# AdaLN modulation columns computed by a multiply-and-sum on VectorE, with most lower weight parts split off on GpSimd

## The chip, the cores and the metric

The kernel runs on one core of a Trainium2 chip, in float32. The metric is the device time of one execution in microseconds (us). The engines are TensorE (PE, matrix products; PEld is its weight load), VectorE (DVE), ScalarE (ACT) and GpSimd (POOL). Weights are fetched by DMA from one queue that SyncE (SP) issues in order.

## The reference

Two transformer blocks over one sequence of 256 tokens and 1024 features. What the change touches is the modulation at the head of each block: one row `c` of 1024 numbers, times a 1024x6144 matrix, gives six vectors.

```
mod = silu(c) @ ada_w + ada_b                       # 6 x 1024
sh1, sc1, g1, sh2, sc2, g2 = split(mod, 6)
h = rmsnorm(x, norm_mix) * (1 + sc1) + sh1
x = x + g1 * (diff_attention(h) @ w_out)            # block 1: qkv = h @ w_in, 8 heads
h = rmsnorm(x, norm_ffn) * (1 + sc2) + sh2
x = x + g2 * hier_moe(h)                            # 16 experts, top 2 of the best group
# then a final rmsnorm, and block 2 in the same shape with c_2, ada_w_2:
# w_in_2, sparse attention and RWKV-7 side by side, w_out_2, MoE of 32 experts
```

## The kernel before

**Layout.** Activations stand feature by feature: 128 features on the partitions, eight column blocks, 256 tokens. The parts sh1, sc1, g1, sh2 and sc2 are therefore wanted as columns (feature on the partition, in the tile `mod`), and only the last gain g2 as a row (`gt`). Memory is cut into 21 units of 128x2048 floats (NU); `Stream` (L98) loads weight tiles of up to 1 MB into slots made of units, each DMA issued on SP (L128) in program order. A load waits until the readers of what its slot held before are done, and everything behind it on SP waits with it.

**Products in three.** A float32 product is done as three faster products on high and lower parts. For block 1's `w_in` and `wo` tiles, `Splits.split` (L619) copies a piece to its high part on ACT (L628) and subtracts for the lower part (L629), on the engine that the plan's letter names: "v" is DVE, "g" is POOL. The plan is "vg": half of each tile on either engine.

**Modulation.** A job is 512 outputs. At the start of block 1, `matvec_rows` (L404) multiplies on PE (L410), ACT copies the row out (L413), PE transposes it (L425) and DVE sums it to columns (L427, L428). From there on `matvecs` (L432) does the jobs beside the heads, by letter: "t" on PE (L467, with an ACT copy), "v" as eight scalar-times-row steps of 128x512 on DVE (L460, then L462). Either leaves rows, which `to_columns` (L481) turns to columns by 128x1 matmuls (L487) and a small DVE sum (L488). In block 2 (parts 2, 4, 3 and the gains) all is "v", with tiles quartered to 128x1024 (0.5 MB) and two slots.

**Stages.** (1) Norm of x and, in two halves over the contraction, the projection to the first half of q, k and v (`first_half`, L746; `ready`, L1370 makes the modulated activation: L587, L591 to L596). (2) From 81 us, `weave` (L137) interleaves the eight heads, `sum_up` (L1404, the modulation jobs, in its last part jobs2(0, 1) for block 2) and `dense` (the rest of the projection, L798, then the first part of the output projection, L908). It orders the work by costs that each generator yields; a negative yield (lead, wait) spends time without work. (3) Output projection and routing from 208 us, then 16 experts from 245 us. (4) Block 2's mixer from 490 to 882 us. There `conditions` weaves the remaining jobs beside selection, heads and RWKV-7. (5) From 882 us on, 32 experts, whose 176 tiles of 1 MB are fetched behind a flag that SP reads (a branch on whether a slot overflowed).

Of the kernel before, what the change touches and what calls it, by code (L numbers as in the profile page):

```python
# [16 lines left out]
P = 128  # L17
# [379 lines left out]

def silu_cond(c, name):
    t = c.const.tile([P, KD], F32, name="cond_" + name)
    c.nc.scalar.activation(t, c.col[name], AF.Silu)  # L400
    return t


def matvec_rows(c, cond, ws):  # L404

    nc = c.nc
    ps = bank(c)
    for k in range(KD):
        g = k % 4
        nc.tensor.matmul(ps[32 * g:32 * g + 32, :], cond[:, k:k + 1].to_broadcast([P, 32]),  # L410
                         ws[k // 4][:, k % 4, :], start=k < 4, stop=k >= 4)
    row = c.small.tile([P, 512], F32, name="mvsum", bufs=1)
    nc.scalar.copy(row, ps)  # L413
    return row


def matvec(c, cond, names, bcol, out):

    nc = c.nc
    for i, nm in enumerate(names):  # L420
        row = matvec_rows(c, cond, [c.st.get(nm + "a"), c.st.get(nm + "b")])
        yield 2.0
        pt = bank(c)
        for b in range(4):
            nc.tensor.transpose(pt[:, b * P:(b + 1) * P], row[:, b * P:(b + 1) * P], c.ident)  # L425
        o = out[:, 4 * i:4 * i + 4]
        nc.vector.tensor_reduce(o, pt.rearrange("p (b g m) -> p b g m", b=4, g=4)[:, :, :, 0], AX.X, ALU.add)  # L427
        nc.vector.tensor_tensor(o, o, bcol[:, 4 * i:4 * i + 4], ALU.add)  # L428
        yield 0.4


def matvecs(c, cond, st, jobs, engs, lead, wait, rows, parts):  # L432

    nc = c.nc
    V = nc.vector
    names = [n + h for n, _ in jobs for h in parts]
    kn = KD // len(parts)
    ahead, left = [], []  # L440

    def sink():
        f, mine, eng = left.pop(0)
        yield from f(mine, c.c32[:, 0:1] if eng == "t" else c.ones[:, 0:1])

    for (_, f), eng in zip(jobs, engs):
        mine = []
        for h in range(len(parts)):
            while names and len(ahead) < len(st.slots):
                ahead.append(st.get(names.pop(0)))  # L450
            yield -lead
            w = ahead.pop(0)
# [20 lines left out]
            if h == 0 and left:  # L473
                yield from sink()
        left.append((f, mine, eng))
        if len(rows) == 1 or f is jobs[-1][1]:
            yield -wait
            yield from sink()


def to_columns(c, bcol, out):  # L481

    def sink(rows, one):
        pt = bank(c)
        for b in range(4):
            for i, row in enumerate(rows):
                c.nc.tensor.matmul(pt[:, b:b + 1], row[:, b * P:(b + 1) * P], one[:row.shape[0]], start=i == 0, stop=i == len(rows) - 1)  # L487
        c.nc.vector.tensor_tensor(out, pt[:, 0:4], bcol, ALU.add)  # L488
        yield 1.2
    return sink  # L490

# [278 lines left out]
def attention1(c, x, o, qkv, ap, sps, pop):  # L770
# [75 lines left out]
    def norm(po, al):  # L846
# [494 lines left out]
def block1(c, xT):  # L1341
    nc, tc, st, I = c.nc, c.tc, c.st, c.I
    mod = c.const.tile([P, 48], F32, name="mod1")
    bcol = c.col["ada_b"]
    cond = silu_cond(c, "c")

    def mv(*parts, hs=(0, 1)):
        for i in parts:
            for h in hs:
                o = slice(8 * i + 4 * h, 8 * i + 4 * h + 4)  # L1350
                yield from matvec(c, cond, [f"ada{2 * i + h}"], bcol[:, o], mod[:, o])
    m = lambda i: mod[:, 8 * i:8 * i + 8]
# [704 lines left out]
def block2(c, acc, out):  # L2057
# [40 lines left out]
    with tc.tile_pool(name="hp2", bufs=1) as hp, tc.tile_pool(name="rp", bufs=1) as rp:  # L2098
# [50 lines left out]
        def conditions():  # L2149
# [88 lines left out]
def tiles():  # L2238

    it = {}
    a = slice(None)

    def w(name, key, *at, k=KD):
        assert name not in it
        it[name] = key, at, k

# [4 lines left out]
    for b, x in (("a", ""), ("b", "_2")):  # L2253
        for i in range(12):
            cs = slice(512 * i, 512 * (i + 1))
            if b == "a" or i < 4:
                for h in range(2):
                    w(f"ad{b}{i}{'ab'[h]}", f"ada_w{x}", (slice(512 * h, 512 * (h + 1)), cs), k=4)
            else:
                for h in range(4):  # L2260
                    w(f"ad{b}{i}{h}", f"ada_w{x}", (slice(256 * h, 256 * (h + 1)), cs), k=2)
    for p in range(3):
# [23 lines left out]
    for pfx, n, x in (("x", 16, ""), ("y", 32, "_2")):  # L2286
# [7 lines left out]
        for q in range(2):  # L2294
# [29 lines left out]
def lay_out(inputs):  # L2324
# [52 lines left out]
def build(tc, I, out):  # L2377
# [4 lines left out]
    with tc.tile_pool(name="const", bufs=1) as c.const, \  # L2382
# [31 lines left out]
```

## Time and profile before

| | us |
|---|---|
| median of 3 runs (lowest to highest) | 1343.98 (1343.59 to 1347.93) |
| the profiled execution: its own time | 1341.36 |
| its span | 1339.8 |

| engine | busy us | share of the span |
|---|---|---|
| PE | 1146.8 | 86% |
| DVE | 592.5 | 44% |
| ACT | 347.0 | 26% |
| POOL | 101.7 | 8% |
| 16 DMA engines | mean 302 GB/s, 404.09 MB | |

The granted TensorE clock was 0.941 of full speed over the span. The busy shares are means over stages with different limits, so they are read stage by stage: a window's row gives the busy time of each engine in that window. A timeline row gives start, duration, engine, line, operation, output<-inputs and shape; xN means N instructions in a run, and what stands in brackets is the idle time before the first and what ended it.

### The profile page before, as it was taken

The numbers are of one execution on the slowest core, as the hardware profiler recorded it, in microseconds if no ns is written. First come the engines' busy times: TensorE is split into PE (matmuls) and PEld (weight loads), VectorE is DVE, ScalarE is ACT, GpSimd is POOL, SyncE is SP. The second block draws the span as 40 slices with busy tenths as digits, with TensorE's granted clock in tenths as the row PEclk, the third lists the DMA queues.
The fourth block names the chain that finished last, engine by engine and source line by source line (L and its number), as shares of the span: only waits on it lengthen the run. The fifth ranks groups of instructions, "written<-read, shape, count | busy, mean of one in ns | idle before, by whom it ended". The sixth has DMA issues, their size and how long they took to land. (4 is left out here: it accounts for less than half of the span.)

```text
span 1339.8 us, 20574 instructions
## 1 busy us (share of the span) xinstructions
PE 1146.8 (86%) x8434; PEld 705.4 (53%) x8434; DVE 592.5 (44%) x1464; ACT 347.0 (26%) x675; POOL 101.7 (8%) x111
## 2 busy tenths in 40 slices
PE   5899977899998986988999999889876797677775
PEld 2777767444434335876788888844332242233221
DVE  4477653333225137698555747343222222222212
ACT  3335331211111124552232224232111111111111
POOL 2421110000001003002410010000000000000000
PEclk7999978899999996999999999989889988999898
DMA  8777756699996953350135628769999999999996
GB/s 302 288 276 267 277 223 274 282 418 419 420 384 246 418 218 123 127 187 34 64 140 208 205 94 331 281 256 417 420 419 420 419 420 420 419 420 418 421 419 267
DMA packets 60516, 404.09 MB, mean 302 GB/s; under 512 B 7328, under 2 KB 7584, under 8 KB 14464
## 3 DMA queue, kind: packets, MB, share of 16 engines
q1 hardware_dynamic: 58464, 400.58, 74.6%
q10 hardware_dynamic: 1824, 2.00, 0.5%
q8 instruction: 68, 1.11, 0.3%
q0 software_dynamic: 128, 0.13, 0.2%
q14 instruction: 32, 0.26, 0.1%
HBM read 401.64 MB, written 1.05 MB: 301 GB/s over the span
## 5 line engine op out<-in xcount | busy, mean ns | idle before, releaser
L1218 PE MATMUL a<-u,u 128*32 128x512 f32 (+1 forms) x1536 | 297.8, 614 | 36.2 <-DMA u<-in_expert_w_up 25.3
L1198 DVE SCALAR_TENSOR_TENSOR gs<-a,gc,gt 128x512 f32<-128x512 f32 (+1 forms) x50 | 37.5, 750 | 367.5 <-PE a L1227 360.2
L1227 PE MATMUL a<-u,hid 128*32 128x512 f32 (+1 forms) x736 | 135.5, 623 | 40.7 <-DMA u<-in_expert_w_down 40.7
L1218 PEld LDWEIGHTS a<-u,u 128*32 128x32 f32 (+1 forms) x1536 | 71.1, 119 | 176.6 <-issue 106.9
L684 PE MATMUL a<-u,u 128*128 128x256 f32 x656 | 141.5, 292 | 1.9 <-DVE u L629 1.9
L684 PE MATMUL a<-u,hi 128*128 128x256 f32 x640 | 136.5, 304 | 0.4 <-ACT u L1531 0.4
L1156 ACT COPY gs<-a 128x512 f32<-128x512 f32 x48 | 28.1, 586 | 335.8 <-PE a L1218 326.1
L684 PEld LDWEIGHTS a<-u,u 128*128 128x128 f32 x656 | 104.4, 193 | 12.7 <-issue 9.2
L684 PEld LDWEIGHTS a<-u,hi 128*128 128x128 f32 x640 | 99.3, 191 | 15.6 <-issue 8.9
L1200 ACT CAST u<-gs 64x512 fp32r<-64x512 f32 x96 | 59.2, 616 | 183.3 <-DVE gs L1198 182.2
L1227 PEld LDWEIGHTS a<-u,hid 128*32 128x32 f32 (+1 forms) x736 | 33.3, 119 | 124.2 <-DMA u<-in_expert_w_down 52.1
L1202 DVE TENSOR_TENSOR u<-gs,u 64x512 fp32r<-64x512 f32 x96 | 65.9, 686 | 27.2 <-ACT u L1200 25.3
L628 ACT CAST hi<-u 128x1024 fp32r<-128x1024 f32 x48 | 49.8, 1047 | 72.0 <-PE a L684 60.0
L629 DVE TENSOR_TENSOR u<-u,hi 128x1024 fp32r<-128x1024 f32 x48 | 61.7, 1291 | 14.7 <-ACT hi L628 14.2
L908 PE MATMUL a<-u,u 128*128 128x256 f32 x256 | 49.0, 312 | 9.2 <-DVE u L629 8.0
L629 POOL TENSOR_TENSOR u<-u,u 128x512 fp32r<-128x512 f32 (+1 forms) x22 | 44.5, 2041 | 127.2 <-ACT u L628 127.2
L1163 PEld LDWEIGHTS a<-sel,gs 128*128 128x128 f32 x256 | 35.1, 212 | 28.4 <-issue 26.3
L1254 PE MATMUL acc<-u,PT 128*128 128x512 f32 x128 | 44.4, 460 | 5.2 <-DVE u L1202 3.6
L1140 PE MATMUL a<-pm,u 128*128 128x256 f32 x256 | 40.8, 315 | 8.1 <-DVE gs L1198 3.2
L908 PEld LDWEIGHTS a<-u,u 128*128 128x128 f32 x256 | 40.4, 216 | 10.3 <-DVE u L629 8.2
L1254 PEld LDWEIGHTS acc<-u,PT 128*128 128x128 f32 x128 | 22.3, 208 | 44.1 <-DVE u L1202 34.3
L763 PE MATMUL e<-u,u 128*128 128x256 f32 x288 | 40.1, 306 | 5.5 <-ACT u L591 5.0
(447 smaller groups left out, 1599.9 us busy)
## 6 DMA issues: line engine op xcount, KB each, us to landing
u<-in_expert_w_gate SPq DMA_DIRECT2D x96, 1024.0 KB, 19.9
u<-in_expert_w_up SPq DMA_DIRECT2D x96, 1024.0 KB, 19.9
u<-in_expert_w_down SPq DMA_DIRECT2D x96, 1024.0 KB, 19.9
u<-in_ada_w SPq DMA_DIRECT2D x32, 1024.0 KB, 6.9
u<-in_w_in SPq DMA_DIRECT2D x19, 1024.0 KB, 4.9
u<-in_ada_w SPq DMA_DIRECT2D x32, 512.0 KB, 3.9
u<-in_attn_w_in SPq DMA_DIRECT2D x12, 512.0 KB, 7.8
u<-in_attn_w_in SPq DMA_DIRECT2D x6, 1024.0 KB, 7.4
```

The lines of the kernel that those rows point to most:

```text
L628: nc.scalar.copy(h[:, o], w[:, o])
L629: (nc.vector if e == "v" else nc.gpsimd).tensor_tensor(l[:, o], w[:, o], h[:, o].bitcast(F32), ALU.subtract)
L684: c.nc.tensor.matmul(ps, a[:, k, c0:c0 + n], b[:, k], start=k == 0 and i == 0, stop=k == kn - 1 and i == 2)
L763: T.matmul(p[:, j * S:(j + 1) * S], l, r, start=(h, j, k, n) == (0, 0, 0, 0), stop=(h, k, n) == (1, 3, 2), skip_group_check=True)
L908: self.c.nc.tensor.matmul(ps[:, j * S:(j + 1) * S], a[:, k, j * P:(j + 1) * P], b[:, k], start=k + j + i == 0, stop=k == KD - 1 and i == 2 ...
L1140: nc.tensor.matmul(ps[:, jj * m:(jj + 1) * m], h[:, t, k * P:(k + 1) * P], pm[:, t], start=i + jj + t == 0, stop=i + t == 2, skip_group_ch ...
L1198: c.nc.vector.scalar_tensor_tensor(out=y[o], in0=py[o], scalar=gc[o], in1=gt[o], op0=ALU.mult, op1=ALU.mult)
L1200: c.nc.scalar.copy(yy[H2[q], q], y[H2[q]])
L1202: c.nc.vector.tensor_tensor(yy[H2[1 - q], q], y[H2[q]], yy[H2[q], q].bitcast(F32), ALU.subtract)
L1218: c.nc.tensor.matmul(pg[r:r + cap], xe[:, k0 + k, x0:x0 + cap], w[:, k, :], start=k0 + k < nk, stop=k0 + k >= KD - nk)
L1227: c.nc.tensor.matmul(py[r:r + cap], hT[:, f], w[:, f - f0, q * 512:(q + 1) * 512], start=f < nk, stop=f >= 4 - nk)
L1254: c.nc.tensor.matmul(acc[:, 2 * t + q], PT[:, t * P:(t + 1) * P], yy[:, q], start=False, stop=stop, skip_group_check=True)
```

## The change

The weights of the column parts (10 of the 12 jobs of each block) are laid out turned: an output feature on the partition and its 1024 inputs along it. `c` and `c_2` are broadcast to all 128 partitions by two DMAs of 0.5 MB on ACT's queue into one more unit (`ucb`; NU is 22), and ACT applies silu there. A block of 128 outputs is then one DVE instruction over 128x1024, which multiplies the weights by the broadcast row in place, sums along the partition and adds the bias, followed by a read of the sum. There are 16 of these in the first stage, 40 beside the heads and 24 in block 2. The gains stay matrix-vector products: both on PE in block 1, both on DVE in block 2. Of the splits of the second half of `w_in` and of `wo`, three of four 128x512 pieces now go to POOL. The jobs for block 2 (jobs2) are woven in only after the fourth norm of heads, and the leads are longer.

```diff
-NU = 21
+NU = 22
 def silu_cond(c, name):
     t = c.const.tile([P, KD], F32, name="cond_" + name)
     c.nc.scalar.activation(t, c.col[name], AF.Silu)
-    return t
-def matvec_rows(c, cond, ws):
-def matvec(c, cond, names, bcol, out):
+    r = c.cb[:, 0 if name == "c" else 1]
+    c.nc.scalar.activation(r, r, AF.Silu)
+    return t, r
+def matvec(c, cb, w, bcol, out):
+    for b in range(w.shape[1]):
+        c.nc.vector.tensor_tensor_reduce(out=w[:, b], in0=w[:, b], in1=cb, scale=1.0, scalar=bcol[:, b:b + 1],
+                                         op0=ALU.mult, op1=ALU.add, accum_out=out[:, b:b + 1])
+def matvecs(c, cb, cond, st, cols, gains, engs, lead, wait, rows, parts):
+    for _, bcol, out in cols:
+        n = 4 // len(parts)
+        for h in range(len(parts)):
+            w = yield from tile()                    # get(...) ahead, then yield -lead
+            matvec(c, cb, w, bcol[:, n * h:n * h + n], out[:, n * h:n * h + n])
-def to_columns(c, bcol, out):
 # block1
-        y = rstd_small(c, token_sum(c, squares(c, xT, KD, np_), KD, np_), D, np_, "rs")
+        ss = token_sum(c, squares(c, xT, KD, np_), KD, np_)
         first = mv(1, 0, hs=[0])
         next(first)
-        nc.vector.tensor_copy(rs, on_features(c, y, np_))
+        ps = on_features(c, rstd_small(c, ss, D, np_, "rs"), np_)
+        next(first)
+        nc.vector.tensor_copy(rs, ps)
-    c.sp = Splits(c, [(f"win{w}{q}", "vg") for q in (2, 3) ...] + [(f"wo{q}", "vg") for q in range(4)],
+    c.sp = Splits(c, [(f"win{w}{q}", "gggv") for q in (2, 3) ...] + [(f"wo{q}", "gggv") for q in range(4)],
-                yield from matvecs(... + gain_jobs(c, "ada", gt), "tvtvtvtvtvtv", 1.25, 3.0, sums, "ab")
+                yield from matvecs(..., gain_jobs(c, "ada", gt), "tt", 2.6, 3.0, sums, "ab")
                 run(late)
-                yield from matvecs(c, c.cond2, st2, c.jobs2((0, 1)), "tvtv", 1.25, 3.0, sums, "ab")
+                while len(normed) < 4:
+                    yield -0.3
+                yield from matvecs(c, c.cb2, None, st2, c.jobs2((0, 1)), [], "", 2.6, 3.0, sums, "ab")
 # block2
-            yield from matvecs(... + gain_jobs(c, "adb", c.gt2), "vvvvvvvv", 0.5, 3.0, rows, "0123")
+            yield from matvecs(..., gain_jobs(c, "adb", c.gt2), "vv", 1.3, 3.0, rows, "0123")
-        un.give(*uth, *c.umasks)
+        un.give(*uth, *c.umasks, c.ucb)
 # build
+            c.ucb = c.un.raw()
+            c.cb = c.ucb.rearrange("p (i k) -> p i k", i=2)
+            nc.scalar.dma_start(c.cb[:, 0], I["c"].partition_broadcast(P))
             nc.sync.dma_start(c.uxT, I["x"])
+            nc.scalar.dma_start(c.cb[:, 1], I["c_2"].partition_broadcast(P))
```

In the three places below, `u_...` are units or slots, `mod_...` is the tile of modulation columns and A the scale made from them. `ISA` at L410 of the new kernel is the multiply-and-sum, with the read of its sum behind it. Lines have moved: L629 is now L599, L587 L557, L596 L566, L1373 L1348, L719 L689.

On DVE, in the second half of the first projection, the columns of sc1 and sh1 were two short sums each; before:

```order
L427 TENSOR_REDUCE mod_115<-a 128x4
L428 TENSOR_TENSOR mod_115<-mod_115,va 128x4
L1373 SCALAR_TENSOR_TENSOR A_173<-mod_115,va 128x4
L587 SCALAR_TENSOR_TENSOR mt<-u_67,A_173,rsx 128x256 x3
L427 TENSOR_REDUCE mod_115<-a 128x4
L629 TENSOR_TENSOR u_126<-u_71,u_126 128x512
L428 TENSOR_TENSOR mod_115<-mod_115,va 128x4
L596 SCALAR_TENSOR_TENSOR u_119<-mt,mod_115,u_118 128x256
```

Now, in the same place:

```order
L410 ISA u_74,mod_118<-u_74,u_80,va 128x1024
L410 ISA mod_118 128x1
L410 ISA u_68,mod_118<-u_68,u_80,va 128x1024
L410 ISA mod_118 128x1
L1348 SCALAR_TENSOR_TENSOR A_163<-mod_118,va 128x4
L557 SCALAR_TENSOR_TENSOR mt<-u_67,A_163,rsx 128x256 x2
L410 ISA u_69,mod_118<-u_69,u_80,va 128x1024
L410 ISA mod_118 128x1
L410 ISA u_69,mod_118<-u_69,u_80,va 128x1024
L410 ISA mod_118 128x1
L566 SCALAR_TENSOR_TENSOR u_123<-mt,mod_118,u_122 128x256
```

Four long instructions stand ahead of A and two more ahead of the first activated block.

On SP, at the end of the heads' stage, the tiles of `wo` (in_attn_w_out) stood among the last modulation tiles; before:

```order
L128 DMA u_72<-in_attn_w_out 128x2048
L128 DMA u_663<-in_ada_w 128x2048
L128 DMA u_664<-in_ada_w 128x2048
L128 DMA u_665<-in_ada_w 128x2048
L128 DMA u_666<-in_ada_w 128x2048
L128 DMA u_663<-in_ada_w 128x2048
L128 DMA u_73<-in_attn_w_out 128x2048
L128 DMA u_70<-in_attn_w_out 128x2048
L128 DMA u_71<-in_attn_w_out 128x2048
```

Now:

```order
L128 DMA u_72<-in_attn_w_out 128x2048
L128 DMA u_73<-in_attn_w_out 128x2048
L128 DMA u_70<-in_attn_w_out 128x2048
L128 DMA u_71<-in_attn_w_out 128x2048
L128 DMA u_611<-in_ada_w 128x2048
L128 DMA u_612<-in_ada_w 128x2048
L128 DMA u_613<-in_ada_w 128x2048
```

All four tiles of `wo` stand ahead of the last eight modulation tiles, which are those of block 2.

On DVE, in block 2, behind the copy of a row of reciprocal roots (L719) for which PE waits, in the selection of the sparse attention (L1912, L1913); before:

```order
L719 COPY u_3449<-gy 128x8x2
L460 TENSOR_SCALAR mvsum<-u_4917,cond_c_672 128x512
L1484 SCALAR_TENSOR_TENSOR u_4435<-a,vb,u_4435 128x255
L1912 MAX m_4419<-u_3944 128x8
L462 SCALAR_TENSOR_TENSOR mvsum<-u_4917,cond_c_672,mvsum 128x512
L1913 MATCH_REPLACE u_3944<-m_4419,u_3944 128x256
L462 SCALAR_TENSOR_TENSOR mvsum<-u_4917,cond_c_672,mvsum 128x512
```

Now:

```order
L689 COPY u_3303<-gy 128x8x2
L410 ISA u_4771,mod_619<-u_4771,u_80,vb 128x1024
L410 ISA mod_619 128x1
L1461 SCALAR_TENSOR_TENSOR u_4289<-a,vb,u_4289 128x255
L1889 MAX m_4273<-u_3798 128x8
L410 ISA u_4771,mod_619<-u_4771,u_80,vb 128x1024
L410 ISA mod_619 128x1
L1890 MATCH_REPLACE u_3798<-m_4273,u_3798 128x256
```

Each long instruction reads a 0.5 MB tile of its own, where such a tile served two short steps before.

## Rows read from the trace of the kernel before

**Rows 1.** The chain that ended last, shares by engine.

```profile
DMA 29%; PE 3%; DVE 1%; ACT 0%; issue 0%; SPq 0%; ACTq 0%; DVEq 0%
```

**Rows 2.** Windows: start:end, length, busy by engine, granted clock, DMA share, GB/s.

```profile
81.30:162.00 80.70, 78.98 (x554) 59.82 (x556) 58.83 (x187) 36.51 (x94) 13.30 (x5) 0.96 0.69 261
162.00:208.00 46.00, 32.96 (x207) 26.95 (x208) 30.42 (x87) 16.53 (x45) 5.13 (x6) 0.79 0.52 206
640.00:660.00 20.00, 20.00 (x229) 15.87 (x231) 10.65 (x28) 6.64 (x16) 8.57 (x9) 1.00 0.03 5
860.00:880.00 20.00, 12.25 (x84) 11.86 (x83) 10.88 (x51) 4.45 (x11) 0.23 (x4) 0.74 0.30 106
900.00:920.00 20.00, 19.33 (x156) 9.03 (x158) 7.79 (x22) 4.20 (x8) 0.00 (x0) 1.00 1.01 418
```

**Rows 3.** Timeline of SP's queue around the experts' branch.

```profile
882.07 0.33 SPq L128 DMA_DIRECT2D u<-in_expert_w_gate  x1
```

**Rows 4.** Timeline: single DVE and POOL instructions, for their prices.

```profile
25.07 1.26 POOL L629 TENSOR_TENSOR u<-u,u 128x512 fp32r<-128x512 f32 x1 [13.94 <-ACT u L628]
78.90 1.23 DVE L629 TENSOR_TENSOR u<-u,u 128x1024 fp32r<-128x1024 f32 x1
82.42 0.42 DVE L818 CUSTOM_DVE_ANT_0 sc<-s,negD 128x256 f32<-128x256 f32 x1
82.76 0.42 DVE L818 CUSTOM_DVE_ANT_0 sc<-s,negD 128x256 f32<-128x256 f32 x1
...
630.02 0.28 DVE L2001 CUSTOM_DVE_ANT_0 u<-a,u 128x128 f32<-128x128 f32 x1
632.12 0.42 DVE L2001 CUSTOM_DVE_ANT_0 u<-a,u 128x256 f32<-128x256 f32 x1
```

**Rows 5.** Timeline of PE, PEld and DVE, start to the first projection's end.

```profile
20.65 0.15 PEld L410 LDWEIGHTS a<-u,cond_c 128*32 128x32 f32 x4 [0.88 <-DMA u<-in_ada_w]
27.60 1.53 PE L763 MATMUL e<-u,u 128*128 128x256 f32 x4 [2.49 <-ACT u L591]
30.73 11.61 DVE L629 TENSOR_TENSOR u<-u,u 128x512 fp32r<-128x512 f32 x7 [0.28 <-ACT u L628]
49.07 1.92 PE L410 MATMUL a<-u,cond_c 128*32 128x512 f32 x16
59.77 17.46 PE L763 MATMUL e<-u,u 128*128 128x256 f32 x134
```

**Rows 6.** Groups of DVE instructions, 81.3 to 162 us: busy, mean ns, idle before.

```profile
L462 DVE SCALAR_TENSOR_TENSOR u<-u,cond_c,u 128x512 f32<-128x512 f32 x28 | 20.9, 747 | 0.4
L629 DVE TENSOR_TENSOR u<-u,u 128x1024 fp32r<-128x1024 f32 x5 | 10.0, 2001 | 0.1
L460 DVE TENSOR_SCALAR u<-u,cond_c 128x512 f32<-128x512 f32 x4 | 3.3, 832 | 0.0
```

**Rows 7.** Groups of PE instructions, 81.4 to 162 us.

```profile
L467 PE MATMUL a<-u,cond_c 128*32 128x512 f32 x70 | 10.0, 621 | 0.0
L487 PE MATMUL a<-c,u 128*128 128x1 f32 x48 | 5.6, 244 | 0.0
L487 PE MATMUL a<-ones,u 128*128 128x1 f32 x24 | 3.0, 244 | 0.1
```

**Rows 8.** Groups of DVE instructions, 162 to 208 us.

```profile
L462 DVE SCALAR_TENSOR_TENSOR u<-u,cond_c,u 128x512 f32<-128x512 f32 x14 | 10.4, 744 | 0.1
```

**Rows 9.** Timeline of PE and POOL, 162 to 208 us.

```profile
176.25 4.90 POOL L629 TENSOR_TENSOR u<-u,u 128x1024 fp32r<-128x1024 f32 x2 [20.05 <-ACT u L628]
183.81 2.29 PE L908 MATMUL a<-u,u 128*128 128x256 f32 x9 [8.04 <-DVE u L629]
```

**Rows 10.** Group of PE instructions in block 2, whole span.

```profile
L487 PE MATMUL a<-ones,mvsum 128*128 128x1 f32 x48 | 5.8, 242 | 0.0
```

**Rows 11.** Timeline of PE in block 2, where it waits for reciprocal roots.

```profile
608.76 0.66 PE L724 MATMUL a<-ident,u 128*128 128x128 f32 x2 [2.72 <-DVE u L719]
```

**Rows 12.** Timeline of PE, the second half of the projection in the heads' stage.

```profile
112.14 2.41 PE L798 MATMUL a<-u,u 128*128 128x256 f32 x18 [0.49 <-ACT aT L838]
```

More of the change, by code (lines that the diff above doesn't have):

```diff
@@ L400, in silu_cond @@
     c.nc.scalar.activation(t, c.col[name], AF.Silu)
-    return t
-def matvec_rows(c, cond, ws):
[L406 to L414, printed above, removed]
-def matvec(c, cond, names, bcol, out):
[L419 to L429, printed above, removed]
@@ L432, in matvecs @@
-def matvecs(c, cond, st, jobs, engs, lead, wait, rows, parts):
+    r = c.cb[:, 0 if name == "c" else 1]
[6 more added lines that the diff above has]
+def matvecs(c, cb, cond, st, cols, gains, engs, lead, wait, rows, parts):
@@ L436, in matvecs, with tile @@
     nc = c.nc
     V = nc.vector
-    names = [n + h for n, _ in jobs for h in parts]
+    names = [n + h for n, *_ in cols + gains for h in parts]
     kn = KD // len(parts)
[L440 to L446, printed above, removed]
+    ahead = []
+    def tile():
+        while names and len(ahead) < len(st.slots):
+            ahead.append(st.get(names.pop(0)))
+        yield -lead
+        return ahead.pop(0)
@@ L447, in matvecs @@
+    for _, bcol, out in cols:
[3 more added lines that the diff above has]
+            matvec(c, cb, w, bcol[:, n * h:n * h + n], out[:, n * h:n * h + n])
+    for (_, f), eng in zip(gains, engs):
         mine = []
         for h in range(len(parts)):
[L449 to L452, printed above, removed]
+            w = yield from tile()
@@ L472, in matvecs @@
                 yield 1.0
[L473 to L478, printed above, removed]
-def to_columns(c, bcol, out):
[L483 to L490, printed above, removed]
+        yield -wait
+        yield from f(mine, c.c32[:, 0:1] if eng == "t" else c.ones[:, 0:1])
 def to_gain(c, gt, q):
@@ L504, in col_jobs @@
 def col_jobs(c, name, parts, bcols, mod):
-    return [(f"{name}{2 * i + h}", to_columns(c, bcols[:, 8 * i + 4 * h:8 * i + 4 * h + 4], mod[:, 8 * i + 4 * h:8 * i + 4 * h + 4]))
+    return [(f"{name}{2 * i + h}", *(v[:, 8 * i + 4 * h:8 * i + 4 * h + 4] for v in (bcols, mod)))
             for i in parts for h in range(2)]
@@ L776, in attention1 @@
     ready = {0, 1}
-    done = []
+    done, normed = [], []
     def wait(h):
@@ L855, in norm @@
         V.tensor_tensor(on, p4, y.unsqueeze(2).to_broadcast([P, 4, P]), ALU.mult)
+        normed.append(on)
         return on
@@ L892, in heads @@
         yield from back(*pend)
-    return proj, heads, done
+    return proj, heads, done, normed
 class Project:
@@ L1344, in block1 @@
     bcol = c.col["ada_b"]
-    cond = silu_cond(c, "c")
+    cond, cb = silu_cond(c, "c")
     def mv(*parts, hs=(0, 1)):
@@ L1349, in mv @@
             for h in hs:
-                o = slice(8 * i + 4 * h, 8 * i + 4 * h + 4)
-                yield from matvec(c, cond, [f"ada{2 * i + h}"], bcol[:, o], mod[:, o])
+                for j in range(2):
+                    o = slice(8 * i + 4 * h + 2 * j, 8 * i + 4 * h + 2 * j + 2)
+                    matvec(c, cb, st.get(f"ada{2 * i + h}{'ab'[j]}"), bcol[:, o], mod[:, o])
+                    yield
     m = lambda i: mod[:, 8 * i:8 * i + 8]
@@ L1380, in block1 @@
     un.give(*his[4:])
-    c.sp = Splits(c, [(f"win{w}{q}", "vg") for q in (2, 3) for w in range(3)] + [(f"wo{q}", "vg") for q in range(4)],
+    c.sp = Splits(c, [(f"win{w}{q}", "gggv") for q in (2, 3) for w in range(3)] + [(f"wo{q}", "gggv") for q in range(4)],
                   [(his[i], his[i + 1]) for i in (0, 2)])
@@ L1400, in block1 @@
             next(late)
-            proj, heads, done = attention1(c, x, (oh, ol), qkv, ap, sps, banks(c, px, 1, "po"))
+            proj, heads, done, normed = attention1(c, x, (oh, ol), qkv, ap, sps, banks(c, px, 1, "po"))
             c.sp.prepare(2)
             def sum_up():
-                yield from matvecs(c, cond, st2, col_jobs(c, "ada", (2, 4, 3), bcol, mod) + gain_jobs(c, "ada", gt), "tvtvtvtvtvtv",
-                                   1.25, 3.0, sums, "ab")
+                yield from matvecs(c, cb, cond, st2, col_jobs(c, "ada", (2, 4, 3), bcol, mod), gain_jobs(c, "ada", gt),
+                                   "tt", 2.6, 3.0, sums, "ab")
                 run(late)
-                yield from matvecs(c, c.cond2, st2, c.jobs2((0, 1)), "tvtv", 1.25, 3.0, sums, "ab")
+                while len(normed) < 4:
+                    yield -0.3
+                yield from matvecs(c, c.cb2, None, st2, c.jobs2((0, 1)), [], "", 2.6, 3.0, sums, "ab")
             def dense():
@@ L2048, in condition2 @@
     mod = c.const.tile([P, 48], F32, name="mod2")
-    c.cond2 = silu_cond(c, "c_2")
+    c.cond2, c.cb2 = silu_cond(c, "c_2")
     c.m2 = lambda i: mod[:, 8 * i:8 * i + 8]
@@ L2156, in conditions @@
             rows = [c.small.tile([P, 512], F32, name="mvsum", bufs=1)]
-            yield from matvecs(c, cond, st2, c.jobs2((2, 4, 3)) + gain_jobs(c, "adb", c.gt2), "vvvvvvvv", 0.5, 3.0, rows, "0123")
+            yield from matvecs(c, c.cb2, cond, st2, c.jobs2((2, 4, 3)), gain_jobs(c, "adb", c.gt2), "vv", 1.3, 3.0, rows, "0123")
             un.give(u)
@@ L2243, in tiles, with w @@
     a = slice(None)
-    def w(name, key, *at, k=KD):
+    def w(name, key, *at, k=KD, turned=False):
         assert name not in it
-        it[name] = key, at, k
+        it[name] = key, at, k, turned
     def cols(name, key, x0, n):
@@ L2254, in tiles @@
         for i in range(12):
[L2255 to L2261, printed above, removed]
+            parts = "ab" if b == "a" or i < 4 else "0123"
+            n = len(parts)
+            for h in range(n):
+                if i < 10:
+                    o = 512 * i + 512 // n * h
+                    w(f"ad{b}{i}{parts[h]}", f"ada_w{x}", (a, slice(o, o + 512 // n)), k=4 // n, turned=True)
+                else:
+                    w(f"ad{b}{i}{parts[h]}", f"ada_w{x}", (slice(D // n * h, D // n * (h + 1)),
+                                                           slice(512 * i, 512 * (i + 1))), k=KD // n)
     for p in range(3):
@@ L2305 @@
          "rwkv_ln_b_2": "ln_b", "kv_norm_g_2": "kvg", "q_norm_g_2": "qg", "k_norm_g_2": "kg"}
-AS_IS = ("ada_b", "ada_b_2", "attn_lam_q1", "attn_lam_k1", "attn_lam_q2", "attn_lam_k2", "rwkv_w2_2", "rwkv_a2_2",
+AS_IS = ("c", "c_2", "ada_b", "ada_b_2", "attn_lam_q1", "attn_lam_k1", "attn_lam_q2", "attn_lam_k2", "rwkv_w2_2", "rwkv_a2_2",
          "rwkv_g2_2", "router_expert_bias_2")
@@ L2350, in lay_out @@
     flat = {}
-    for key, at, k in tiles().values():
-        flat.setdefault(key, []).append(block(np.concatenate([one[key][i] for i in at], axis=1)).reshape(-1))
+    for key, at, _, turned in tiles().values():
+        t = np.concatenate([one[key][i] for i in at], axis=1)
+        flat.setdefault(key, []).append(block(t.T if turned else t).reshape(-1))
     r.update((key, np.concatenate(v)) for key, v in flat.items())
@@ L2359, in weights @@
     r, pos = {}, {}
-    for name, (key, at, k) in tiles().items():
-        n = k * sum(width(key, i) for i in at)
+    for name, (key, at, k, turned) in tiles().items():
+        n = k * (D if turned else sum(width(key, i) for i in at))
         x = pos.get(key, 0)
@@ L2392, in build @@
         with tc.tile_pool(name="ld", bufs=1) as lp:
+            load_vectors(c)
+            c.ucb = c.un.raw()
+            c.cb = c.ucb.rearrange("p (i k) -> p i k", i=2)
+            nc.scalar.dma_start(c.cb[:, 0], I["c"].partition_broadcast(P))
             nc.sync.dma_start(c.uxT, I["x"])
-            load_vectors(c)
+            nc.scalar.dma_start(c.cb[:, 1], I["c_2"].partition_broadcast(P))
             setup(c, lp)
@@ L2402 @@
     from concourse.bass_utils import run_bass_kernel_spmd
-    nc = bacc.Bacc("TRN2", target_bir_lowering=False, num_devices=1)
+    nc = bacc.Bacc("TRN2", target_bir_lowering=False, num_devices=1, dynamic_dma_scratch_size=4096)
     arrays, aps = {}, {}
```

## The prediction

> **What bounds the kernel now.** I read the chain of waits first: 29% of the span is waiting for DMA, and it lies at the end, in block 2's experts [rows 1]. There the windows show a plain limit: 418 GB/s and a DMA share of 1.01, with DVE at 7.8 of 20 us (window 900 to 920) [rows 2]. Those loads hang on a flag and start at 882 us [rows 3]; just before it the DMA share is 0.30 in the window 860 to 880 [rows 2]. So all that happens before 882 us passes through to the end one for one, and what is saved after it is nothing unless it is a load. The change works almost wholly before 882 us. Next the windows by stage. While the heads run (81 to 162 us) PE is busy 79.0 of 80.7 us and DVE 58.8: PE is the bound, with DVE some way behind. From 162 to 208 us neither is full (33.0 and 30.4 of 46): the stage is a chain of waits. In block 2 PE is full from 640 us on (20.0 of 20.0) [rows 2].
>
> **The price of the new instruction.** No row shows a multiply-and-sum over 128x1024. The same kind over 128x256 (L818) starts every 0.34 us with the read of its sum in between (82.42, 82.76). A custom DVE operation takes 0.28 us for 128 columns and 0.42 for 256, so 1.09 ns for a column. One instruction over 1024 with its read: 0.34 + 768 x 1.09 ns = 1.18 us. A subtraction of the same size with two inputs in SBUF takes 1.23 us, which says the same. As a lower end I take 1.14 (1024 columns and the fixed part), as an upper end 2.3 us, twice that, because the L818 rows have one input in PSUM and cannot tell what two SBUF inputs and a sum do together [rows 4]. I take 1.18, nearest to the row of equal size. A block of 512 outputs is 4 x 1.18 = 4.7 us; on DVE before it was 3.3/4 + 7 x 0.747 = 6.1 us [rows 6].
>
> **1. Start to the end of the first projection: +1.5 (-3 to +6).** First half: the first matmul is at 27.60 us, and the last modulation tile lands at 20.65 [rows 5]. Two broadcasts of 0.5 MB now go ahead of it, 1.05 MB at 418 GB/s = 2.5 us, so 23.2. Two multiply-and-sums (2.4) follow, then what stands behind them on DVE: the rest of the norm's chain (about 1.0), its spread over the partitions through PE and back (about 1.7), a product (0.4), split pieces between them (about 2) and the activation (0.5). That gives 31.2 to 31.7, some 4 us late. But the gap between the halves is paid for by DVE: it ends its splits at 42.34 (30.73 + 11.61), and PE sits from 49.07 to 59.77 over matrix-vector products, transposes and the wait for their columns [rows 5]. With the splits at 46.3, eight multiply-and-sums are 9.4, and A, four products, three lower parts and two split pieces about 5 to 6: the second half starts at 60.9 to 62.2. Against 59.77 I take +1.5: the matrix-vector products that leave PE there give nothing, because DVE is late instead. The bounds are a DVE queue that overlaps more of the first half's splits (-3) and one that adds a stall at each (+6).
>
> **2. Heads, 81 to 162 us: -8 (-14.6 to 0).** PE loses about two of the four jobs and a bit in its 10.0 us of L467 (the two gains stay; I take off 4.3) and the column turns, 5.6 and 3.0: 12.9, so 79.0 becomes 66.1 [rows 2, 7]. DVE loses 20.9 + 3.3 of scalar steps, 10.0 of splits and about 1 of small sums, and gains 24 x 1.18 = 28.3, six split pieces of about 0.6 (3.7), and stalls by POOL. Those I take from the rows: five DVE splits take 2.00 us on average instead of 1.23, so 3.9 us are lost to 13.3 us of POOL's splits [rows 2, 4, 6]. POOL now has 18 pieces of 1.26 = 22.7 us, so 6.7. DVE: 58.8 - 35.2 + 38.7 = 62 us, up to 65 since neighbours' times overlap a little. So PE and DVE end near 66 and 63, both almost full and both in order, each waiting for the other at every tile. Such a pair does not reach its floor; the bounds are 66.1 (-14.6) and the old 80.7 (0), and I take the middle, 73. ACT, with four copies for two of twice the size, has 36.5 of 80.7 busy and hides it.
>
> **3. 162 to 208 us: -7 (-11 to +3).** PE stands 8.04 us at 183.81 for a lower part of `wo`; POOL starts its two halves at 176.25, after 20 us of idling for a high part [rows 9]. That is a late tile: in the order the four tiles of `wo` now stand ahead of the last eight modulation tiles, and a tile's DVE share is a quarter. DVE loses 10.4 and two first steps (1.0) and some 2.4 of splits, and gains 16 x 1.18 = 18.9: 30.4 becomes 35.5 [rows 2, 8]. That fits into 46 - 8 = 38, but tightly, with four multiply-and-sums inside the last head's norm. I take -7, most of the stall; the ends are all of it with the column turns too (-11) and a stall that DVE gives back with interest (+3).
>
> **4. Block 2's mixer: -1 (-6 to +6).** The column turns, 5.8 us, leave PE [rows 10], and PE is the bound where most of them stood. Against it: two slots, a 0.5 MB load for each instruction, and these stand on DVE between the reciprocal roots for which PE already waits 2.72 us at 608.76 [rows 11]; in the same stretch eight now stand. A slot's turn-round is its load (1.25 us at 418 GB/s), its issue and the instruction, 4 to 5 us for two; where DVE meets an unloaded tile, those behind it wait. I put that at +4.5.
>
> **5. One more free unit at the branch: -2.5 (-2.5 to 0).** `ucb` comes back before 882, so 17 loads of the experts stand ahead of the flag instead of 16. One tile of 1.05 MB is 2.5 us, in a stretch whose DMA share is 0.30 [rows 2].
>
> **Sum.** +1.5 - 8 - 7 - 1 - 2.5 = -17. The profiled execution took 1341.36: 1324.4. The median of the runs is 2.6 above it, so 1327.
>
> **Rivals.**
>
> B. The heads reach PE's floor, since nothing but matmuls is left there. For it: PE had 1.7 us of gaps in 80.7 while DVE did 58.8 [rows 2]. Against: DVE's long instructions now hold back short ones (scores, norms) that PE waits for. Heads -14.6, the next stage -11, block 2 -6: 1311.
>
> C. DVE and POOL shut each other out. For it: the 2.00 against 1.23 us [rows 4, 6]. If every POOL piece stops DVE for its whole length, 22.7 takes the place of 6.7 in step 2; DVE is then at 78 to 81 us, the stage's old length, and terms 2 and 3 give nothing: 1342. Against: the present loss is 3.9 of 13.3, not all of it.
>
> D, on the slower side. The multiply-and-sum runs at half rate, 2.2 us, because both inputs are in SBUF. One us more each: +10 at the start (eight in a row where DVE is the bound, two before the first half), DVE in the heads 62 + 24 = 86 to 90, so +10 instead of -8; +9 in the next stage instead of -7; +4 in block 2 instead of -1; together 1376. It decides from about 1.8 us on, where DVE passes the old 80.7 (62 + 24 x 0.6 = 77, and the overlaps). Against: L462 reads two SBUF inputs at 747 ns for 512 columns and the subtraction 1.23 for 1024, neither halved [rows 4, 6], but neither sums. [...]
>
> E. Loads come late. SP issues in order, and the second half of `w_in` now stands behind modulation tiles whose slots wait for DVE. The projection in the heads' stage reads its next tile at 112.14 with 0.49 us of wait [rows 12], so there is slack of little. Four tiles late by 6 us (two tiles at 2 x 1.18, and the transfers) would be 24: 1351. Against: the longer lead puts DVE's work further behind its load.
>
> **How the numbers follow.** The forecast A (1327) gets 0.53, B 0.13, C 0.18, D 0.09, E 0.07. A's own range is 1316 to 1338, from the halves of the bounds of terms 2 to 4. For 8 in 10 I go to B below and C above: 1310 to 1344. A measurement of this kernel tells 0.3% (4 us) from no change. A and B are faster; C half of the time, a third the same; D and E are slower but for a small part of E: faster 0.75, same 0.08, slower 0.17.
>
> **What would show it.** The multiply-and-sum at 1.2 us right, 2.2 D. The first matmul of block 1 near 31.5 and its second half near 61. The heads' stage 73 us long with PE near 66 busy; no wait of 8 us on a lower part in L908's successor. DVE splits well over 1.3 us for 128x512 mean C. In block 2 a longer wait at the reciprocal roots and fewer idle us after 640. The first loads of the second experts' stage 17 before the branch, and the branch near 867. The forecast is wrong if the stage of the heads does not shorten by 4 us or more.

## The result and the profile after

The changed kernel takes 1355.43 us (median of 5 runs, 1354.06 to 1358.98) against 1343.98 (5 runs, 1342.67 to 1347.93): the ratio is 1.0085, 95% interval 1.0061 to 1.0108. It is slower, by less than 1%; 1327 was forecast, and the range ended at 1344. Of the profiled execution the span is 1353.5 us, 13.7 longer.

Where the time went shows best in how late the same PE instructions start. Each number is the median of (start there - start in the kernel before), over the PE instructions that both have and that start in 15 us of the kernel before; the experiments, told below, stand beside it. e8 leaves work out, so its row is to be read up to 240 us only.

| from us (before) | 60 | 210 | 315 | 390 | 480 | 570 | 645 | 750 | 840 | 1305 |
|---|---|---|---|---|---|---|---|---|---|---|
| after | +0.1 | -5.5 | -5.9 | 0.0 | +5.4 | +6.4 | +17.7 | +11.7 | +13.8 | +12.3 |
| e1 order pinned | -1.8 | -4.6 | -4.9 | -4.9 | -3.8 | -2.8 | +8.5 | +2.6 | +4.7 | +3.3 |
| e2 block 2 alone | -0.5 | -1.1 | -1.1 | -1.1 | -1.1 | -1.1 | +9.1 | +3.1 | +6.3 | +8.8 |
| e3 pinned, sums late | -1.7 | -6.1 | -6.5 | -6.5 | -5.5 | -4.5 | -3.6 | -11.4 | -7.3 | -9.1 |
| e5 heads held | -0.9 | -4.3 | +4.8 | +4.8 | +5.7 | +6.6 | +7.5 | -0.3 | +3.6 | +1.9 |
| e8 quarter sums | -1.2 | -18.5 | -18.9 | -18.9 | -18.9 | -18.9 | -19.2 | -27.0 | -23.1 | -24.7 |

Two losses stand out in the first row: 11.3 us inside block 1's experts (315 to 480), where nothing was edited, and 11.3 us in block 2's mixer (570 to 645), of which 6.0 come back by 750.

**The new instruction** ([rows 4] answer). DVE at the start; columns start, duration:

```profile
14.18 1.28 DVE L410 CUSTOM_DVE_ANT_0 u<-u,u,va 128x1024 f32<-128x1024 f32 x1
15.38 0.08 DVE L410 DVE_READ_ACCUMULATOR2_ANT mod<- 128x1 f32 x1
15.38 1.28 DVE L410 CUSTOM_DVE_ANT_0 u<-u,u,va 128x1024 f32<-128x1024 f32 x1
```

One follows the other every 1.20 us; 1.18 was forecast, and half rate (rival D) would have been 2.2. Both inputs of this sum are in SBUF, and it is not halved.

**Start to the first projection's end** ([rows 5] answer). PE:

```profile
32.94 20.52 PE L733 MATMUL e<-u,u 128*128 128x256 f32 x144 [2.12 <-ACT u L561]
...
63.11 14.24 PE L733 MATMUL e<-u,u 128*128 128x256 f32 x104 [0.76 <-DVE u L566]
```

The first matmul starts 5.3 us late (27.60 before), but the projection ends where it did (63.11 + 14.24 = 77.35; before 59.77 + 17.46 = 77.23), since 40 of the second half's 144 matmuls already ran in the gaps between 54.26 and 63.11. The second half of before starts at 58.18; the 59.77 of [rows 5] is where a window cut the run:

```profile
58.18 19.05 PE L763 MATMUL e<-u,u 128*128 128x256 f32 x144 [2.54 <-ACT u L591]
```

**Heads** ([rows 2, 6] answer). Windows, columns as in [rows 2], and PE's waits from 80 to 215 us (waiter, releaser, us, times, longest):

```profile
82.00:164.00 82.00, 69.51 (x449) 53.94 (x449) 69.94 (x208) 39.02 (x113) 27.13 (x19) 0.86 0.71 280
164.00:210.00 46.00, 27.73 (x166) 24.17 (x167) 38.82 (x95) 11.74 (x36) 9.03 (x10) 0.78 0.56 215
100.00:120.00 20.00, 12.11 (x68) 8.86 (x66) 20.00 (x56) 9.59 (x29) 9.27 (x6) 0.78 0.67 267
```

```profile
PE a L834 <- DVE on L825: 21.9, 4, 9.0
PE s L781 <- DVE u L713: 6.3, 1, 6.3
PE a L806 <- DVE u L711: 3.7, 1, 3.7
PE s L781 <- DVE mx L788: 2.4, 2, 1.2
```

The 8.04 us wait for a lower part [rows 9] is gone. In its place PE waits 21.9 us, four times, for the normed heads; before it was

```profile
PE a L863 <- DVE on L855: 3.7, 1, 3.7
```

DVE is full from 100 to 120 us. Its groups from 82 to 164 us, three of now and one of before:

```profile
L410 DVE CUSTOM_DVE_ANT_0 u<-u,u,va 128x1024 f32<-128x1024 f32 x23 | 31.1, 1360 | 0.0
L794 DVE SCALAR_TENSOR_TENSOR sc<-sc,rt 128x256 f32<-128x256 f32 x13 | 8.7, 674 | 0.0
L599 DVE TENSOR_TENSOR u<-u,u 128x512 fp32r<-128x512 f32 x7 | 7.2, 1026 | 0.9 <-ACT u L598 0.9
```

```profile
L824 DVE SCALAR_TENSOR_TENSOR sc<-sc,rt 128x256 f32<-128x256 f32 x12 | 5.8, 479 | 0.0
```

What holds a norm (L489, L490, L824, L825) shows on DVE:

```profile
178.35 0.15 DVE L489 SCALAR_TENSOR_TENSOR onz<-onz,onv 128x4 f32<-128x4 f32 x1
...
178.49 1.27 DVE L410 CUSTOM_DVE_ANT_0 u<-u,u,vb 128x1024 f32<-128x1024 f32 x1
...
179.69 0.15 DVE L490 SCALAR_TENSOR_TENSOR ony<-onz,ony 128x4 f32<-128x4 f32 x1
179.76 1.27 DVE L410 CUSTOM_DVE_ANT_0 u<-u,u,vb 128x1024 f32<-128x1024 f32 x1
...
180.97 0.15 DVE L824 TENSOR_TENSOR ony<-ony,al 128x4 f32<-128x4 f32 x1
181.04 1.27 DVE L410 CUSTOM_DVE_ANT_0 u<-u,u,vb 128x1024 f32<-128x1024 f32 x1
...
182.25 0.68 DVE L825 TENSOR_TENSOR on<-po,ony 128x512 f32<-128x512 f32 x1
```

Each step of 0.15 us stands behind a sum of 1.27, while PE idles 8.97 us for the last of them (to 183.07).

**Block 1's experts.** The code is the same, but the compiler's scheduler, which orders each engine's instructions over the whole block, gave PE another order. Between two experts, from the programs (lines as in the new kernel), before and after:

```
before: L1189 | L1215 acc x4 | L1154 gate x2 | L1215 acc x4 | L1189 ...
after:  L1189 | L1215 acc x8 | L1152 transpose x2 | L1154 gate x2 | L1189 ...
```

PE's three longest waits from 322 to 486 us, before and after; the second line of the new ones is a wait that the kernel before does not have:

```profile
PE acc L1244 <- DVE u L1202: 4.5, 8, 1.6
PE a L1140 <- DVE gs L1198: 3.2, 1, 3.2
PE a L1140 <- DVE hid L1168: 1.3, 2, 0.7
```

```profile
PE acc L1215 <- DVE u L1173: 4.4, 7, 0.6
PE a L1152 <- DVE gc L1158: 3.0, 5, 0.7
PE a L1111 <- DVE gs L1169: 2.2, 1, 2.2
```

SP's queue goes still for longer where the stream gives up three slots and waits for PE to free the rest: 22.7 us before, 29.4 after, 22.3 in e1. So the loss comes in two halves: PE falls back 5.9 us up to 390 us, while the queue is still ahead of the kernel before, and 5.4 more behind the pause, out of which the loads come 1.3 us late where they went in 5.4 us early. SP of before, of after and of e1:

```profile
390.78 0.33 SPq L128 DMA_DIRECT2D u<-in_expert_w_up  x1
413.46 0.33 SPq L128 DMA_DIRECT2D u<-in_expert_w_gate  x1
```

```profile
385.34 0.33 SPq L128 DMA_DIRECT2D u<-in_expert_w_up  x1
414.71 0.33 SPq L128 DMA_DIRECT2D u<-in_expert_w_gate  x1
```

```profile
386.35 0.33 SPq L128 DMA_DIRECT2D u<-in_expert_w_up  x1
408.68 0.33 SPq L128 DMA_DIRECT2D u<-in_expert_w_gate  x1
```

**Block 2** ([rows 11] answer). PE at the second reciprocal root, and DVE ahead of and behind it:

```profile
621.18 0.66 PE L694 MATMUL a<-ident,u 128*128 128x128 f32 x2 [6.01 <-DVE gh L2172]
```

```profile
614.84 1.37 DVE L410 CUSTOM_DVE_ANT_0 u<-u,u,vb 128x1024 f32<-128x1024 f32 x1
...
616.91 1.27 DVE L410 CUSTOM_DVE_ANT_0 u<-u,u,vb 128x1024 f32<-128x1024 f32 x1
...
619.65 1.28 DVE L410 CUSTOM_DVE_ANT_0 u<-u,u,vb 128x1024 f32<-128x1024 f32 x1
...
622.15 1.28 DVE L410 CUSTOM_DVE_ANT_0 u<-u,u,vb 128x1024 f32<-128x1024 f32 x1 [1.01 <-DMA u<-in_ada_w]
...
625.70 1.28 DVE L410 CUSTOM_DVE_ANT_0 u<-u,u,vb 128x1024 f32<-128x1024 f32 x1 [2.26 <-DMA u<-in_ada_w]
```

Three sums stand inside the root's chain (PE waits 6.01 us, before 2.72), and the next two hold DVE 3.3 us for their tiles. Another 2.4 us are the clock: 24 matmuls behind the first root take 5.47 us where they took 3.11, at a granted clock of 0.50 (window below):

```profile
596.50:602.00 5.50, 5.50 (x26) 5.50 (x27) 4.26 (x11) 0.37 (x1) 0.00 (x0) 0.50 0.88 295
```

PE had idled 3.71 us ahead of it, as long as before, where the clock stayed at 1.00 (590.0 to 593.2 us); why it fell here is open. With the same edit in block 2 and the same idle of 3.71 us these matmuls took 3.11 us in e2 and 4.20 in e1, so this part does not come with the edit each time.

### The profile page after: what moved, and what is told of

Its sections match the earlier page's. It is cut to its first block, busy times and chain, and to the rows that moved or that the text cites. A ratio compares the mean times of both kernels' runs of the same rounds, so it can differ in the third digit from the quotient of the medians.

```text
span 1353.5 us, 20011 instructions
## 1 busy us (share of the span) xinstructions
PE 1114.5 (82%) x8124; PEld 687.0 (51%) x8124; DVE 624.8 (46%) x1504; ACT 344.7 (25%) x685; POOL 122.9 (9%) x131
## 5 line engine op out<-in xcount | busy, mean ns | idle before, releaser
L1198 PE MATMUL a<-u,hid 128*32 128x512 f32 (+1 forms) x736 | 130.2, 610 | 44.5 <-DMA u<-in_expert_w_down 44.5
L654 PE MATMUL a<-u,u 128*128 128x256 f32 x656 | 141.3, 295 | 2.2 <-DVE u L599 2.2
L654 PEld LDWEIGHTS a<-u,u 128*128 128x128 f32 x656 | 106.6, 198 | 8.1 <-issue 4.6
L1198 PEld LDWEIGHTS a<-u,hid 128*32 128x32 f32 (+1 forms) x736 | 31.1, 118 | 126.0 <-DMA u<-in_expert_w_down 58.4
L599 POOL TENSOR_TENSOR u<-u,u 128x512 fp32r<-128x512 f32 x42 | 60.9, 1472 | 106.8 <-ACT u L598 98.0
L599 DVE TENSOR_TENSOR u<-u,hi 128x1024 fp32r<-128x1024 f32 x48 | 61.3, 1284 | 17.7 <-ACT hi L598 17.5
L410 DVE CUSTOM_DVE_ANT_0 u<-u,u,vb 128x1024 f32<-128x1024 f32 x40 | 53.6, 1352 | 3.9 <-DMA u<-in_ada_w 3.9
L410 DVE CUSTOM_DVE_ANT_0 u<-u,u,va 128x1024 f32<-128x1024 f32 x40 | 53.9, 1363 | 0.1
L598 ACT CAST u<-u 128x512 fp32r<-128x512 f32 (+1 forms) x72 | 43.4, 653 | 24.3 <-DMA u<-in_attn_w_in 5.2
L879 PE MATMUL a<-u,u 128*128 128x256 f32 x256 | 45.8, 300 | 0.0
```

The lines of the kernel that those rows point to most:

```text
L410: c.nc.vector.tensor_tensor_reduce(out=w[:, b], in0=w[:, b], in1=cb, scale=1.0, scalar=bcol[:, b:b + 1], op0=ALU.mult, op1=ALU.add, accum_ ...
L598: nc.scalar.copy(h[:, o], w[:, o])
L599: (nc.vector if e == "v" else nc.gpsimd).tensor_tensor(l[:, o], w[:, o], h[:, o].bitcast(F32), ALU.subtract)
L654: c.nc.tensor.matmul(ps, a[:, k, c0:c0 + n], b[:, k], start=k == 0 and i == 0, stop=k == kn - 1 and i == 2)
L879: self.c.nc.tensor.matmul(ps[:, j * S:(j + 1) * S], a[:, k, j * P:(j + 1) * P], b[:, k], start=k + j + i == 0, stop=k == KD - 1 and i == 2 ...
L1198: c.nc.tensor.matmul(py[r:r + cap], hT[:, f], w[:, f - f0, q * 512:(q + 1) * 512], start=f < nk, stop=f >= 4 - nk)
```

## The experiments

The kernel before was timed beside each set: 1343.11 (e1 to e4), 1344.73 (e5 to e7) and, a single run, 1343.69 us (e8). Times of different sets are best compared by their ratios to it, which the text gives with their 95% intervals.

**e1.** The changed kernel; order edges in the experts' stage alone (the table of the order of before and the helper that applies it are left out here).

```diff
+        start = len(nc.cur_bb.bb.instructions)
         experts(c, "x", 16, (th, tl), slot, gate, add, 64, ep, gt, {14: ahead})
+        pin_order(c, start)   # on PE, DVE, ACT: each behind the one that preceded it before
```

> The changed kernel with one thing held: inside block 1's expert stage, PE, DVE and ACT issue their instructions in exactly the order that they had in the kernel before (same instructions, order edges only). Theory O (the new order in the expert stage is what costs there): the stage no longer falls behind; the 11.4 us between 325 and 480 us come back, the time is about 1344 to 1346 and block 2 starts some 6 us earlier than in the kernel before, not 5.5 later. Rival L (the loads or the clock make the stage late, the order is only a sign of it): the loss stays, about 1355.

Measured: 1343.96 us (10 runs), 1.0018 of before (1.0001 to 1.0035). The stage keeps its -4.9 up to 420 us and ends at -3.8, where some -6 was expected. Theory O: the same instructions in another order cost 9 to 11 us of the whole. The medians, of two sets, differ by 1355.4 - 1344.0 = 11.4 us; the ratios by 0.0067, or 9.0 us; the traces by 10.2 within the stage (11.3 lost against 1.1) and by 9.0 at 1305 us. Block 2's edit alone leaves the experts' order as it was (e2 runs the whole stage at -1.1); which of the other edits changes it, no run shows. Which wait of the new order costs how much is not resolved; all waits of PE that the profile names in the stage sum to 11.6 us, before to 9.0.

**e2.** The kernel before with block 2's edit alone (turned weights for its six jobs, the broadcasts, the extra unit).

> The kernel before with the change in block 2's mixer alone (multiply-and-sum there, the broadcast of c and c_2 and the extra unit with its return before the last experts); start, heads and splits as before, and the expert stage of block 1 has the order of before. Theory W (block 2 loses by itself: multiply-and-sums between the reciprocal roots and behind half-megabyte loads): 585 to 645 us fall behind by 9 to 11 us, some 6 come back by 760, the branch is 6 to 9 us later, less 2.3 for the returned unit, and the broadcasts cost up to 4 at the start: 1347 to 1353. Rival S (block 2's loss in the changed kernel came with the late and reordered stage ahead of it): no loss there, 1342 to 1345.

Measured: 1350.48 us (9 runs), 1.0074 (1.0047 to 1.0101), as theory W expected: from -1.1 at 570 to +9.1 at 645, and back to +3.1 at 750. After 840 it loses 5.6 more up to the branch, which the other kernels do not (e1: 1.0); this is not explained. The broadcasts cost nothing by 60 us (-0.5).

**e3.** e1, and block 2's sums held in program order on DVE.

```diff
+        if w.shape[1] == 1:                      # block 2's quartered tiles
+            c.tc.keep_in_program_order(i)        # i: the multiply-and-sum
```

> As e1, and block 2's multiply-and-sums are held on DVE behind what was written ahead of them, which puts all 24 behind the three reciprocal-root copies, into the stretch where PE is full. Theory W: the waits at these copies fall back to those of before (2 to 4 us each), 6 to 9 us less than e1, about 1336 to 1339. Rival: DVE in the later stretch becomes late for RWKV-7 and nothing is won, or the slow part is PE's clock and not the instructions: within 2 us of e1.

Measured: 1334.53 us (9 runs), 0.9937 (0.9914 to 0.9961): faster than both kernels, and faster than the 1336 to 1339 expected. PE's waits from 560 to 660 us:

```profile
PE a L696 <- DVE u L691: 8.5, 3, 3.7
PE a L2013 <- POOL u L2006: 0.5, 1, 0.5
```

These are before's 8.5 us; the mixer goes from -4.5 at 570 to -3.6 at 645 and, with the column turns gone from PE and no sum in the way, to -11.4 at 750.

**e4.** e1 with the splits "vg" again.

> As e1, but the splits of the second half of w_in and of wo are again half on DVE, half on POOL (two 128x1024 pieces instead of four of 128x512). [...] Theory D (DVE itself is full: multiply-and-sums at 1.36 us each instead of 1.18): giving DVE twice the split work lengthens the heads' stage by 3 to 6 us, 1348 to 1351. [...]

Measured: 1344.05 us, 1.0012 (0.9996 to 1.0028), -4.5 at 210 as e1's -4.6. The 3 to 6 us of theory D did not come: in sum it is worth nothing here which engine does the splits. Two things offset each other: DVE's own splits take 10.0 us instead of 7.2, and the multiply-and-sum's mean falls from 1362 to 1339 ns with half of POOL's work (14.1 us for 27.9). So e4 does not tell that POOL's work costs DVE nothing:

```profile
L410 DVE CUSTOM_DVE_ANT_0 u<-u,u,va 128x1024 f32<-128x1024 f32 x24 | 31.7, 1339 | 0.3 <-issue 0.3
L599 DVE TENSOR_TENSOR u<-u,u 128x1024 fp32r<-128x1024 f32 x7 | 10.0, 1429 | 2.6 <-ACT u L598 2.6
```

**e5, e6.** e3 with the sums beside the heads held in program order too (e6: leads 1.25 and 0.6, no wait for the norms).

> As e3, and the multiply-and-sums beside the heads are held on DVE behind what was written ahead of them too. In e3's heads' stage PE waits 23.3 us, in four places, for the normed heads (L827); 17 multiply-and-sums stand inside these four chains of short instructions, here 3. Theory N (PE's new wait is these chains): the four waits fall from 23.3 to under 10 us and the stage ends some 8 to 12 us earlier; but all 16 multiply-and-sums for block 2 stand behind the last chain here, 19 us on DVE, and the experts' first loads queue on SP behind their tiles, which takes some back: 1324 to 1332. Rival F (DVE is simply full, the order of its work does not matter): within 2 us of e3, 1332 to 1336.

> As e5, with short leads (1.25 and 0.6 in place of 2.6) and without the wait for the fourth norm, so that the last multiply-and-sum stands ahead of the last two norms and none is left for the end of the stage; 6 stand inside one chain. Theory N: the stage as in e5 or a little later, but the tiles of block 2 leave SP's queue earlier, so the experts start earlier: 1322 to 1330, not above e5. Rival: the DVE work that is moved forward makes the first heads late by as much, at or above e5.

Measured: 1340.79 us, 0.997 (0.9953 to 0.9988), and 1342.58 us, 1.0001 (0.9981 to 1.0022): both slower than e3 and than e7, which was timed beside them. PE's waits from 80 to 215 us in e5 and in e6:

```profile
PE a L836 <- DVE on L827: 13.3, 4, 5.6
PE s L783 <- DVE u L715: 6.9, 1, 6.9
PE a L656 <- DVE u L601: 6.2, 1, 6.2
```

```profile
PE s L783 <- DVE mx L790: 18.3, 3, 10.1
PE s L783 <- DVE u L715: 5.5, 1, 5.5
PE a L836 <- DVE on L827: 5.1, 2, 3.9
```

The wait for the norms shrinks (23.3 to 13.3 and 5.1; theory N said under 10), and comes back at lower parts (6.2) or at scores (18.3): at 210 us PE is 1.8 us later than in e3 in e5 (-4.3 against -6.1), and 9.8 later in e6 (+3.7). So the stage is not 8 to 12 us shorter, and theory N's forecast falls. But most of e5's loss comes behind the heads, from -4.3 at 210 to +4.8 at 315, where the out projection's result waits on DVE behind the 16 sums for block 2, as the expectation feared; and while those sums waited for the last norm, DVE was busy for only 26.9 of 46 us. PE's wait from 205 to 320 us and that window, in e5:

```profile
PE acc L933 <- DVE u L904: 7.5, 2, 5.4
164.00:210.00 46.00, 36.84 (x234) 26.95 (x233) 26.93 (x78) 18.01 (x52) 12.41 (x13) 0.93 0.63 250
```

So these are two orders that failed, and not proof that none helps.

**e7.** e3 without the unit's return.

> As e3, but the unit of the broadcasts is not given back ahead of block 2's experts: 16 loads instead of 17 stand ahead of the flag. Step 5 (one load more in an idle stretch is worth its transfer): the last experts end 2 to 3 us later than in e3, 1336 to 1338. Rival: the loads ahead of the flag are not the bound, no difference (1333 to 1335).

Measured: 1335.76 us, 0.9952 (0.9934 to 0.9969). Up to 885 us it runs with e3, 0.8 us ahead of it (-6.8 and -6.0); at 1305 it is 2.1 later. That fits step 5; the times of the two sets alone do not tell e7 from e3, as their intervals overlap.

**e8.** e3 with the sums beside the heads over 256 inputs.

```diff
+    if part:                                     # beside the heads
+        w, cb = w[:, :, :D // 4], cb[:, :D // 4]
```

> As e3, but the 40 multiply-and-sums beside the heads read only 256 of their 1024 inputs (this leaves three quarters of those sums out; the same tiles are loaded, as many instructions issued). Theory F (DVE is what the heads' stage waits for): some 40 x 0.9 = 36 us of DVE work are gone, PE's waits for normed heads and scores fall from some 37 us to under 15, and the out projection ends 10 to 20 us earlier than in e3. Rival E (the weight tiles come late on SP's queue) or rival Q (PE's own order is the limit): the stage is as long as in e3 within 3 us. Only the stages up to 240 us are read, since later routing depends on the values.

Measured in one trace: at 210 us it is 12.4 ahead of e3 (-18.5 against -6.1), and PE's 23.3 us for normed heads are 9.3; all its waits fall from 37 to 22 us, not under 15. Theory F: what the heads' stage waits for is the sums' time on DVE. A quarter sum is also a shorter thing to stand behind, so e8 does not part the amount of work from the length of each sum.

## Why the prediction was wrong

- **Price and start.** 1.20 us for 1.18: right. +0.1 for +1.5 is near in size, partly by luck. The first half starts 1.4 us later than forecast and the second half's long run 2, and 40 matmuls in the gaps, which the sum did not have, pay it back. Step 1 also took the second half's start from a row that a window had cut (59.77 for 58.18), and its own terms give 60.7 to 61.7 us, not 60.9 to 62.2.
- **Steps 2 and 3** gave -5.6 together (+0.1 to -5.5) for -15, a term too large by 9.4. The heads' stage itself gave some 3 us of it (-3.4 at 150 us), less than the 4 us below which the prediction called itself wrong. The late tile of `wo` did go, and PE did lose its work. But DVE was put at 62 to 65 us busy and "almost full" was treated as a floor that the two engines could reach half way to. DVE was busy for 69.9 of 82 us. The sums and the splits cost what was forecast, stalls included (31.1 + 7.2 us for 28.3 + 3.7 + 6.7), but short steps of the heads were stalled too, which had no term (L794 takes 674 ns on average, where its L824 took 479 before), and each short step of a norm or a score stood behind a sum while PE waited (e8). Rival C's mechanism is part of this: what DVE's instructions that overlap a piece on POOL take above the median of their kind sums to some 10.4 us from 82 to 164 us (an estimate from the trace; 5.3 before), less than half of the 22.7 that C charged. By the same count e4, with half of POOL's work, has 7.3 us, so it did not take these stalls away.
- **Not in the sum: block 1's experts.** The prediction said that the change works before 882 us and passes on one for one, and gave the stage from 241 to 482 us no term. It read the new order only around the edits. The order of PE there had changed: the stage lost 11.3 us, and e1, which gives back the old order, loses 1.1 there. This term, put at nothing without a reason, is the first step that failed; the oversized steps 2 and 3 and step 4 are the others, of about the same weight (9.4 us off each).
- **Step 4** had the right mechanism and the wrong size. Forecast: 5.8 won on PE, 4.5 lost; measured: 11.3 lost and 6.0 won back by 750, some 8 in all by 840 (5.4 to 13.8), outside -6 to +6. e3 shows that nearly all the loss is where the sums stand.
- **Step 5**, -2.5: 2.1 by e7's trace, in line with it.

With these, -17 becomes +0.1 - 5.6 + 11.3 + 8.4 - 1.5 = +12.7 at 1305 us (the table's +12.3, as another 0.4 is won from 210 to 315; 13.7 at the end). The forecast's own range for A does not follow from its words: the halves of the bounds of terms 2 to 4 give 1319 to 1340, not 1316 to 1338. Neither reaches the measured time.

## What to carry to other kernels

When a scheduler orders the whole program, compare the order of every stage before and after, also of those that nobody edited, and give a stage whose order moved a term of its own. An instruction that is cheap by its sum is dear where it stands between the short steps of a chain that another engine waits for; hold it behind them if that engine has slack later (e3: 1334.53 us for e1's 1343.96). Where it has little slack, ask what stands behind the held work in turn: in e5 it was the out projection (7.5 us of waits), and the two orders tried there only moved the wait (e5, e6).

## What the runs showed that was not expected

The same instructions in another order cost 9 to 11 us in a stage where the DMA share is 1.01 for most of its length (250 to 384 us, before and after). And 24 matmuls ran at a granted clock of 0.50 once, after an idle of 3.71 us that left it at 1.00 in the kernel before.

A sum that overlaps a subtraction on POOL took nearly twice as long: in e5 six in a row take 2.3 us each, where the one ahead of them takes 1.28, while six pieces on POOL take 2.2 us each (1.26 alone [rows 4]). DVE and POOL in e5:

```profile
125.16 1.28 DVE L410 CUSTOM_DVE_ANT_0 u<-u,u,va 128x1024 f32<-128x1024 f32 x1
126.36 2.31 DVE L410 CUSTOM_DVE_ANT_0 u<-u,u,va 128x1024 f32<-128x1024 f32 x1
125.49 13.22 POOL L601 TENSOR_TENSOR u<-u,u 128x512 fp32r<-128x512 f32 x6 [8.93 <-ACT u L600]
```
